# One decoder layer on eight cores: output and input in pieces, sample steps moved later, token segments joined, one normalisation paced

## The chip, the cores and the metric

The kernel runs on all 8 cores of one Trainium2 chip. Each core works on its own prompt of 2048 tokens and its own 16 sample sequences of one token each; there is no traffic between cores. The metric is the time on the device of the slowest core, in microseconds (us). Some executions fall in a slow state: the records of one die, or of both, show a lower granted TensorE clock (for example 0.923 to 0.926 on one die against 0.992 to 0.993 on the other). A median and the range in brackets are of all runs of a kernel, slow ones included; every ratio, and every profile read here, is of fast runs alone.

## The reference, cut to what matters

```python
# model width 1024, FFN width 2816, 4 GLA heads of 128 x 256
x = x + 0.5 * swiglu(rmsnorm(x, g_ffn1), w_ffn1_in, w_ffn1_out)      # "ffn1"
h = rmsnorm(x, g_mix)
u_a, v_a, q_b, k_b, v_b, g_b, lr_b, gate_a, gate_b = split(h @ w_in)
v_n = layernorm(gelu(v_a));  y_a = gelu(u_a) * (tril(W_s) @ v_n + b)  # "m1": spatial gating, chunks of 128
o, s_new = gla_recurrence(q, k, v, log_a, s0)                         # state (4, 128, 256) per sequence
y_b = rmsnorm_head(o) * silu(g_b)
mix = sigmoid(gate_a) * (y_a @ w_proj_a) + sigmoid(gate_b) * (y_b @ w_proj_b)
x = x + mix @ w_out
x = x + 0.5 * swiglu(rmsnorm(x, g_ffn2), w_ffn2_in, w_ffn2_out)      # "ffn2"
x = x + (p @ w_ple) * sigmoid(rmsnorm(x, g_ple) @ w_ple_gate)        # "ple"
y = rmsnorm(x, g_final)
```

For the 16 sample sequences of a core the recurrence is one step: a state of 512 KB is loaded, decayed, given `k^T v`, stored as an output, and multiplied by `q`. That makes 8 MB in and 8 MB out per core beside the weights.

## The kernel before

The prompt is cut into four subs of 512 tokens, worked in two pairs (A, B). In the first pair A carries the 16 sample tokens as well (528 columns, as segments of 256 and 272). For each pair the stages run in the order ffn1, m1 and the rest of the mixer, ffn2, ple; TensorE ("PE") takes its instructions in the order in which the host program emitted them (before, core 1, it stood 22.40 us until 906.02 in front of eight one-column matmuls that waited for a state copy, with matmuls of 512 columns behind them). The other engines are ACT (ScalarE: Square, Sigmoid, Ln, Exp and the like, with table loads in between: 78 of 1283 ns mean in the profile before), DVE (VectorE: element-wise work), POOL (GpSimd: some of the adds) and SP, which only issues transfers. Matmul results go to the banks of PSUM (`ps` in the profiles); the program lets ACT or DVE read a bank out (an "eviction") before PE writes it again. The "DMA share" is the mean busy share of the core's 16 DMA engines.

That order comes from a list scheduler. The main program emits the large matmuls ("foreground"). Everything else is a Python generator, spawned as a task, that yields the model time after which it wants to go on: norms, sample steps, the final norm with its stores. Before each foreground matmul group the tasks that are due are run:

```python
def pe(self, fn, reads, writes, dur):            # every group of matmuls goes through here
    if not self.in_bg:
        self.run_bg()                            # tasks due by now emit their instructions first
        ... # then: run further tasks for as long as the operands are not ready
    idx = p.add("pe", fn, reads, writes, dur=dur)
    ...
    return idx
```

The norm: ACT squares each chunk of x, DVE adds the squares, one matmul with ones sums over partitions, ACT makes Ln and Exp of it (1/rms), DVE multiplies eight chunks.

```python
def rinv_of(acc, segs, adds, dst=None):
    ...
    for (c0, n, _, _) in segs:                   # one round per token segment
        for t in adds[c0]:
            yield from after(t)
        ... # matmul with ones, ACT Ln, ACT Exp
    return r

def xn_of(S, gc, src, segs, r, pace=0.0):
    for (c0, n, _, _) in segs:
        yield K.until(r.k(0, c0, n), margin=-200.0)
        for kc in range(KC):                     # 8 multiplies on DVE
            K.stt(S.xn(kc, c0, n), src(kc, c0, n), col(gc + kc), r(0, c0, n), ALU.mult, ALU.mult, ...)
            if kc % 2:
                yield pace                       # 0: all eight in one burst
    ...
```

The sample steps share one state buffer for even and one for odd sequences. Their loads and stores, and the stores of y, go out on the queue of the SP engine, in order; here a transfer that waited held everything behind it (before, core 1: SP issued nothing from 851.76 to 876.32 us, 24.5 of it spent waiting for the y store to land).

```python
def samples():
    ...
    t0 = K.now                                   # spawned as pair 1 starts
    for n_ in range(NS):
        s0 = s0b[n_ % 2]
        yield max(K.until(s0.k(), ...), t0 + SPACE * (n_ + 1) - K.now)     # SPACE = 13500 ns
        ... # 4 matmuls k^T v, 4 DVE updates of s0
        K.dma("sp", ss_d[n_]..., s0.ap, ..., nbytes=524288)   # store the state
        K.act(snb.ap, s0.ap, AF.Copy, ...)                    # bf16 copy
        if n_ + 2 < NS:
            load_s0(n_ + 2)                                   # next load into the same buffer, at once
        ... # 8 one-column matmuls that read snb
```

The last task of a sub multiplies x and stores it; for the first pair in one piece, and reloads x for the next pair in one piece:

```python
def final_task(S, segs, chunked, nxt, adds, pace):
    ...
            for kc in range(KC):
                K.stt(S.x(kc, c0, n), ...)
                if chunked:
                    K.dma("sp", y_d[S.s][:, kc, ...], ...)
                yield pace
    ...
        if not chunked:
            K.dma("sp", y_d[S.s], S.x.ap[:, :, 0:PT], ..., nbytes=1 << 21)
        if nxt is not None:
            K.dma("sp", nxt.x.ap[:, :, 0:PT], x_d[nxt.s], ..., nbytes=1 << 21)
```

## Time and profile before

The median of five runs was 1669.62 us (1665.83 to 1878.98). The profiled execution was a fast one; its cores spanned 1658.0 to 1666.1 us at a mean granted clock of 0.979 to 0.984.

I split the span at the first matmul of each stage, recognised in the timeline by its operand tiles (for example, the first matmul that reads the low-rank weights begins m1). Medians over the eight cores:

| stage | length, us | of it PE idle, us |
|---|---|---|
| start, up to the first real matmul | 20.7 | 16.6 |
| pair 0: ffn1 | 239.9 | 0.0 |
| pair 0: m1 of A / of B | 21.7 / 18.2 | 2.8 / 0.0 |
| pair 0: rest of mixer and ffn2 | 477.0 | 9.6 |
| pair 0: ple | 37.4 | 3.5 |
| pair 1: ffn1 | 272.7 | 26.1 |
| pair 1: m1 of A / of B | 18.7 / 18.9 | 2.4 / 0.0 |
| pair 1: rest of mixer and ffn2 | 469.2 | 5.4 |
| pair 1: ple | 53.0 | 11.9 |
| after the last ple matmul | 13.2 | 12.6 |

Read it by comparing equal work: the two ffn1 stages differ by 33 us, though the first has 16 columns more to work on and the second only the sample steps beside it (16 times some 0.65 us of matmuls, about 10 us); the two ple stages differ by 16. This is the timeline of core 1 around the first m1, PE only (columns: start, duration, engine and line, operation, tiles, count, and in brackets the idle time before it with what ended it):

```profile
283.40 2.62 PE L45 MATMUL ps<-s_xn,s_wlr 128*16 128x512 bf16 x8 [2.67 <-DVE s_xn L472]
```

B's first m1 matmuls wait 2.67 us for B's normalised x.

### The profile page before, as it was taken

How to read it: one execution, taken by the hardware profiler on the slowest of the kernel's cores; microseconds unless marked ns; L12 is line 12 of the kernel's file. 1: busy time of each engine (PE TensorE's matmuls, PEld its weight loads, DVE VectorE, ACT ScalarE, POOL GpSimd, SP SyncE). 2: the span in 40 equal slices, each digit the busy share in tenths (PEclk: the TensorE clock that was granted, in tenths of full speed). 3: DMA queues.
4: the chain of work that ended last, by engine and by line, in shares of the span. 5: the costliest groups of instructions: out<-in, count | busy, mean ns of one | idle time of the engine just before them, and what ended most of it. 6: DMA issues, size and time to landing. Idle time of an engine off the chain costs nothing.

```text
span 1666.1 us, 23013 instructions; the slowest of 8 cores (1658.0 to 1666.1 us)
## 1 busy us (share of the span) xinstructions
PE 1572.5 (94%) x9323; PEld 878.3 (53%) x9323; DVE 676.8 (41%) x1311; ACT 557.2 (33%) x989; POOL 200.3 (12%) x279
## 2 busy tenths in 40 slices
PE   5999999999899999999984999999999999999985
PEld 4576764655664444444431444444454476667653
DVE  3322236545623521123941333465364263222256
ACT  3321123644722531113530222237355242111145
POOL 3000001101122000001500000010012210000023
PEclk9999999999999999999997999999999999999998
DMA  9753543440524872537497666525341291524403
GB/s 192 110 90 52 89 76 65 77 77 13 90 36 68 152 137 42 97 63 161 71 209 206 176 146 150 122 51 93 60 78 38 51 151 32 97 52 89 77 1 103
DMA packets 65501, 155.67 MB, mean 93 GB/s; under 512 B 6322, under 2 KB 28482, under 8 KB 57716
## 3 DMA queue, kind: packets, MB, share of 16 engines
q0 software_dynamic: 34304, 113.31, 40.2%
q1 hardware_dynamic: 30260, 39.76, 7.8%
q8 instruction: 73, 1.20, 0.3%
q10 hardware_dynamic: 832, 1.14, 0.2%
q14 instruction: 32, 0.26, 0.1%
HBM read 248.01 MB, written 17.40 MB: 159 GB/s over the span
## 4 chain that ended last, share of the span: by engine, by line
PE 83%; DMA 6%; DVE 5%; ACT 4%; issue 2%; ACTq 0%; SPq 0%; DVEq 0%
PE ps L393 48%; PE ps L45 35%; DMA y<-s_x 2%; DMA ss_out<-s_s 2%; DVE s_xn L472 2%; ACT L451 1%; ACT s_tmp L451 1%; DMA s_s<-st 1%; DMA s_x<-x 1%; DVE s_Sf L472 1%; DVE s_x L472 1%; DVE s_ar L472 0%; DVE s_acc L460 0%; ACT s_sq L451 0%; DVE s_tmp L460 0%
## 5 line engine op out<-in xcount | busy, mean ns | idle before, releaser
L393 PE MATMUL ps<-s_xn,s_ring 128*128 128x512 bf16 (+2 forms) x2896 | 613.5, 339 | 0.0
L45 PE MATMUL ps<-s_xn,s_ring 128*128 128x512 bf16 (+2 forms) x2448 | 523.7, 337 | 14.1 <-ACT s_tmp L451 6.5
L451 ACT ACTIVATE s_tmp<-ps 128x512 f32<-128x512 f32 (+2 forms) x448 | 224.9, 512 | 590.6 <-PE ps L393 558.6
L393 PEld LDWEIGHTS ps<-s_xn,s_ring 128*128 128x128 bf16 x2896 | 282.8, 99 | 216.5 <-issue 5.4
L393 PE MATMUL ps<-s_ar,s_ring 128*128 128x512 bf16 (+2 forms) x1957 | 378.3, 341 | 0.0
L45 PEld LDWEIGHTS ps<-s_xn,s_ring 128*128 128x128 bf16 x2448 | 238.9, 99 | 196.5 <-ACT s_tmp L451 8.5
L460 DVE TENSOR_TENSOR s_ar<-s_tmp,ps 128x512 bf16<-128x512 f32 (+1 forms) x220 | 127.7, 583 | 410.1 <-PE ps L393 376.4
L393 PEld LDWEIGHTS ps<-s_ar,s_ring 128*128 128x128 bf16 x1957 | 191.2, 98 | 153.7 <-issue 1.7
L451 ACT ACTIVATE s_sq<-s_x 128x512 bf16<-128x512 f32 (+3 forms) x159 | 83.3, 535 | 227.4 <-DVE s_x L472 207.7
L472 DVE SCALAR_TENSOR_TENSOR s_x<-ps,s_x 128x512 f32<-128x512 f32 (+1 forms) x120 | 70.1, 587 | 183.7 <-PE ps L393 183.7
L45 PE MATMUL ps<-s_ar,s_ring 128*128 128x512 bf16 (+2 forms) x603 | 128.7, 330 | 2.6 <-DVE s_ar L472 2.2
L451 ACT ACT_TABLE_LOAD x78 | 100.1, 1283 | 16.9 <-DMA s_x<-x 9.0
L480 POOL DMA_DIRECT2D s_ring<-w_ffn_in x60 | 41.4, 724 | 379.0 <-PE ps L393 372.3
L472 DVE SCALAR_TENSOR_TENSOR s_xn<-s_x,s_cols,s_rinv 128x512 bf16<-128x512 f32 (+2 forms) x144 | 82.0, 639 | 1.9 <-ACT s_rinv L451 1.9
L45 PEld LDWEIGHTS ps<-s_ar,s_ring 128*128 128x128 bf16 x603 | 58.3, 98 | 45.6 <-DVE s_ar L472 4.5
L460 DVE TENSOR_TENSOR s_acc<-s_acc,s_sq 128x512 bf16<-128x512 bf16 (+2 forms) x147 | 58.9, 402 | 37.0 <-ACT s_sq L451 36.7
L45 PE MATMUL ps<-s_ring,s_xn 128*128 128x512 bf16 (+1 forms) x280 | 64.1, 382 | 0.0
L463 POOL TENSOR_TENSOR s_x<-s_tmp,s_x 128x256 f32<-128x256 f32 (+2 forms) x48 | 47.8, 1012 | 86.5 <-DVE s_tmp L460 78.6
L472 DVE SCALAR_TENSOR_TENSOR s_tmp<-s_tmp,ps 128x512 f32<-128x512 f32 (+1 forms) x40 | 23.2, 581 | 79.8 <-PE ps L393 75.6
L451 ACT ACTIVATE s_ar<-ps 128x512 bf16<-128x512 f32 (+2 forms) x52 | 28.8, 563 | 72.8 <-PE ps L45 53.6
L480 POOL DMA_DIRECT2D s_ring<-w_ffn_out x24 | 12.8, 533 | 301.0 <-PE ps L393 301.0
L463 POOL TENSOR_TENSOR s_ar<-s_tmp,s_ar 128x512 bf16<-128x512 f32 (+1 forms) x40 | 38.3, 960 | 81.5 <-DVE s_tmp L472 81.5
(138 smaller groups left out, 841.2 us busy)
## 6 DMA issues: line engine op xcount, KB each, us to landing
s_ring<-w_ffn_in POOLq DMA_DIRECT2D x36, 1024.0 KB, 17.1
s_ring<-w_in POOLq DMA_DIRECT2D x24, 1024.0 KB, 10.8
s_ring<-w_ffn_out POOLq DMA_DIRECT2D x16, 1024.0 KB, 10.6
s_s<-st SPq DMA_DIRECT2D x16, 512.0 KB, 4.7
ss_out<-s_s SPq DMA_DIRECT2D x16, 512.0 KB, 8.6
s_ring<-w_ffn_out POOLq DMA_DIRECT2D x8, 768.0 KB, 10.3
s_ring<-w_ffn_in POOLq DMA_DIRECT2D x16, 256.0 KB, 15.4
s_ring<-w_ffn_in POOLq DMA_DIRECT2D x8, 512.0 KB, 6.6
```

The source lines that it names most:

```text
L45: ins = self._e.matmul(*a, **k)
L393: ins = e.matmul(o, l, r, start=s, stop=t)
L451: return self.p.add("act", lambda e: e.activation(out, in_, func, scale=scale, **kw), reads, writes, dur=dur)
L460: return self.dve(lambda e: e.tensor_tensor(out, a, b, op), reads, writes, self.size(out), rate)
L463: return self.p.add("pool", lambda e: e.tensor_tensor(out, a, b, op), reads, writes, dur=200.0 + 2.1 * self.size(out))
L472: return self.dve(lambda e: e.scalar_tensor_tensor(out, a, s, b, op0, op1), reads, writes, self.size(out))
L480: return self.p.add(eng, lambda e: e.dma_start(out=out, in_=in_, allow_slow_non_contiguous=slow), reads, writes, dma_sem=sem, extra=extra, ...
```

## The change

The intent was to smooth background work: no 2 MB bursts on the SP queue, the sample steps out of the way of that traffic, background tasks run more eagerly where the main program has short groups, fewer and wider small operations, no burst of eight normalisations in front of evictions, and an earlier start. The diff, cut to its core:

```diff
-SPACE = 13500.0
+SPACE = 12000.0
@@ pe(): eager rule
+        if not self.in_bg and p.stage.startswith(("ple", "m1")):
+            self.run_bg()
@@ norms: one wait and one operation for both token segments; pace for B ahead of ffn2 and ple
-            for (c0, n, _, _) in segs:
-                for t in adds[c0]:
-                    yield from after(t)
+            for t in adds:
+                yield from after(t)
+            for (c0, n, _, _) in segs:
 ...
-            for (c0, n, _, _) in segs:
-                yield K.until(r.k(0, c0, n), margin=-200.0)
+            c0, n = span(segs)
+            yield K.until(r.k(0, c0, n), margin=-200.0)
 ...
-                            sq_feed(adds[S.s, c0], acc_t[S.X], c, c0, n, S.x)
+                        sq_feed(adds[S], acc_t[S.X], c, *span(S.segs), S.x)
 ...
+                        norm_task(S, gnext, adds[S], 1200.0 if S.X == 1 and gnext == C_GPLE else 0.0)
 ...
+            norm_task(S, C_GFFN2, adds, 1200.0 if S.X == 1 else 0.0)
@@ m1: A's spatial step waits for B's norm
             def spat():
+                yield from after(other)
@@ samples(): later, and the next load after the copy's matmuls
-            t0 = K.now
+            t0 = K.now + 90000.0
 ...
-                if n_ + 2 < NS:
-                    load_s0(n_ + 2)
                 yield K.until(snb.k())
                 ... # the 8 one-column matmuls
+                if n_ + 2 < NS:
+                    yield 0.6 * SPACE
+                    load_s0(n_ + 2)
@@ final_task(): y and the reload of x in pieces of 256 KB; for the last B halves PE sums the squares
+                    K.dma("sp", y_d[S.s][:, kc, c0:c0 + np_], S.x(kc, c0, np_), ..., nbytes=512 * np_)
+                    if nxt is not None and kc > 0:
+                        reload(nxt, kc - 1)
                     yield pace
 ...
+                    pss = PS.alloc() if len(halves) > 1 else None
-                    final_task(S, sg, last, N, adds, 400.0 if last else 2500.0)
+                    final_task(S, sg, N, adds, 400.0 if last else 5000.0, pss)
@@ start: order of the first loads, samples last, weights behind the second piece of x
-        x0 = [load_x("sp", A, 0, 2, share=1.7)]
-        K.dma("act", tgs.ap, xs_d, "xis", writes=[tgs.k()])
-        x0 += [load_x("act" if k0 % 4 else "sp", A, k0, 2, share=1.7) for k0 in range(2, KC, 2)]
+        x0 = [load_x("act" if k0 % 4 else "sp", A, k0, 2, share=1.7) for k0 in range(0, KC, 2)]
+        K.dma("sp", tgs.ap..., xs_d..., "xis", writes=[tgs.k()])
 ... # norm_first(): prompt columns first, the sample columns' squares after them
```

## The prediction

> **What bounds the kernel now.** I read the page's head first, then the busy time in stretches of 20 us, then who TensorE (PE) waits for, the chain that ended last, and the timeline at the two worst places.
>
> ```profile
> span 1666.1 us, 23013 instructions; the slowest of 8 cores (1658.0 to 1666.1 us)
> PE 1572.5 (94%) x9323; PEld 878.3 (53%) x9323; DVE 676.8 (41%) x1311; ACT 557.2 (33%) x989; POOL 200.3 (12%) x279
> ```
>
> TensorE is the bound on average: in most stretches it is busy 20.00 of 20.00 us with 94 or so matmuls of 512 columns, one per 213 ns. The change removes no such matmul, so all it can win is the 1666.1 - 1572.5 = 93.6 us in which PE stands still, and the time in which PE runs at a lower clock. The stretches show where those are.
>
> ```profile
> core 1: us, PE busy (x) PEld busy (x) DVE busy (x) ACT busy (x) POOL busy (x), PEclk, DMA share, GB/s
> ...
> 280.00:300.00 20.00, 17.34 (x89) 7.86 (x87) 18.96 (x47) 4.61 (x9) 3.73 (x9) 0.91 0.13 34
> ...
> 880.00:900.00 20.00, 3.63 (x17) 1.47 (x15) 0.00 (x0) 0.00 (x0) 1.48 (x2) 0.71 1.03 235
> 900.00:920.00 20.00, 13.98 (x67) 6.15 (x68) 6.55 (x14) 4.70 (x7) 0.00 (x0) 0.77 0.73 243
> ...
> 1600.00:1620.00 20.00, 15.52 (x122) 12.36 (x121) 12.92 (x27) 11.13 (x26) 9.04 (x12) 0.89 0.00 1
> 1620.00:1640.00 20.00, 16.90 (x138) 13.59 (x136) 9.38 (x25) 15.78 (x36) 7.98 (x11) 0.94 0.03 9
> 1640.00:1660.00 20.00, 9.28 (x54) 6.09 (x54) 17.47 (x44) 7.86 (x20) 7.80 (x10) 0.74 0.43 139
> ```
>
> Around 880 every compute engine is nearly idle while the DMA share is 1.03: PE waits for a transfer. In the last 60 us DMA is empty and DVE, ACT and POOL are half busy: these are waits between engines. Who is waited for:
>
> ```profile
> PE ps L45 <- ACT s_snb L451: 27.6, 3, 22.4
> PE ps L45 <- ACT s_sq L451: 13.9, 3, 11.5
> PE ps L45 <- DVE s_xn L472: 11.2, 4, 4.2
> PE ps L45 <- DVE s_tmp L460: 10.1, 6, 4.0
> PE ps L45 <- ACT s_tmp L451: 7.7, 8, 2.2
> PE ps L45 <- DVE s_acc L460: 5.7, 2, 5.2
> ```
>
> The first row is the sample work: the bf16 copy of a sequence's state, made by ACT. The chain of waits says what that stood behind:
>
> ```profile
> 851.00 25.30 DMA y<-s_x
> 877.00 17.60 DMA ss_out<-s_s
> 894.67 8.46 DMA s_s<-st
> ```
>
> So the 2 MB store of y holds the SP queue until 876, the 2 MB reload of x goes out there, the state store behind it takes 17.6 us instead of its median 8.6, and only then may the next state load start. PE, which runs in program order, stands for 22.4 us in front of eight one-column matmuls. On the other cores the same row totals 19.8 to 28.4 us.
>
> The tail, from the timeline:
>
> ```profile
> 1610.23 6.01 DVE L472 SCALAR_TENSOR_TENSOR s_xn<-s_x,s_cols,s_rinv 128x512 bf16<-128x512 f32 x8
> 1616.65 0.41 PE L45 MATMUL ps<-s_ring 128*128 128x272 bf16 x1 [4.04 <-DVE s_tmp L460]
> 1617.08 1.06 PE L45 MATMUL ps<-s_xn,s_ring 128*128 128x256 bf16 x4
> 1617.93 1.06 PE L393 MATMUL ps<-s_xn,s_ring 128*128 128x256 bf16 x4
> 1658.40 0.39 PE L45 MATMUL ps<-s_acc,s_ones_b 128*128 128x256 bf16 x1 [5.19 <-DVE s_acc L460]
> ```
>
> Eight normalisations of the B half go through DVE in one burst, the evictions of A stand behind them, PE idles 4.04 us, and afterwards four 256-column matmuls start 0.85 us apart where they had 0.44: half clock.
>
> [...]the granted clock falls to 0.5 after the 4.04 us gap, for 6.8 us, and after the 22.4 us gap.[...] SP issues nothing between the y store at 851.00 and the reload at 876.32.[...] The trace has 78 loads of 1283 ns mean, seven of them in the last 65 us.
>
> **The change part by part** (core 1).
>
> *y stores and x reloads in pieces, sample steps later.* The first pair's y (2 x 2 MB) and the reloads (2 x 2 MB) become 32 pieces of 256 KB, one store and one reload per 5 us in place of two 2 MB bursts per half. The sample steps start 90 us later, at about 930 instead of 843, and come every 12 instead of 13.5 us; the next state load is issued 7.2 us after the step, when the 8.6 us store is nearly done, so SP no longer stands in front of it. Two halves overlapping ask for 2 x 105 = 210 GB/s for some 20 us; stretches at 235 to 243 GB/s exist, and the reload of x is not read before the output stage at about 1010. The stall of 27.6 us goes, and with it the slow clock: eight matmuls took 3.45 us after the first gap and about 3.1 after the second, against 1.73. That is 1.7 + 1.4 = 3.1. Sum -30.7.
>
> *Tail.* Idle there: 0.43 + 4.04 + 1.32 + 1.20 + 0.58 + 0.33 + 1.75 + 2.22 + 5.19 + 7.34 = 24.4 us, plus slow clock. (a) The B normalisation is paced 1.2 us per two tiles: the 4.04 goes down to about 1 and the 3 us of slow clock after it go: -6. (b) The two token segments of A share one wait, one square, one add and one final multiply (528 wide). The two pairs of Ln and Exp now follow each other, which saves two table switches of 1.28 us each; the gaps 1.32 and 1.20 hang on them: -2.5. (c) The squares of the last B halves are summed by TensorE in PSUM: 14 adds on DVE of 0.28 go, 16 matmuls of 256 columns come (16 x 0.107 = 1.7 us of PE). DVE is busy 17.47 of 20 us in that stretch and causes the gaps 0.58 + 0.33 + 1.75 + 2.22 = 4.9, with about 2.3 us of slow clock behind them: about -5 + 1.7. (d) The end chain, 5.19 + 7.34, keeps sigmoid, multiply, add, square, matmul, Ln, Exp, eight multiplies and a store; about -1, as a new table load may stand in it. Together -12.8; I take -12, because ACT (about 10 us of work per B half, against 8.5 on PE) then limits.
>
> *m1.* B's first matmul waits 2.67 us in pair one and 2.42 in pair two for B's normalised x. Background work now runs after each matmul group in this stage, ahead of the next Gelu, and A's spatial step waits for B's norm. I expect most of it back: -4.
>
> *First pair's ple stage.* Gaps 1.86 + 1.18 + 0.47 = 3.5; pacing takes the first: -2. The burst for the next pair's normalisation stays.
>
> *Start.* PE does real work from 22.18. The small sample input (64 B runs) moves from the front of ACT's queue to the end of SP's, and weights wait for the second x piece. The last x piece may land 1 to 1.5 us sooner; a sample square and eight small matmuls enter the chain, about +0.5: -0.7.
>
> *Given back.* The sample steps now run until about 1112, through m1 and into the gates of pair two, each with four DVE operations of 0.4 us, one ACT copy of 1.06 us and two PSUM banks beside the one they hold: +2.
>
> Sum: -30.7 - 12 - 4 - 2 - 0.7 + 2 = -47.4, so core 1 ends at 1618.7. Other cores lose less of the stall but start lower (core 0: 1658.0 - 19.8 - 3 - 16.7 = 1618.5), so the slowest is about 1619 to 1620. The reported time is some 1.7 us above the span (1667.81 against 1666.1) and the median another 1.8: about **1623 us**, 2.8% faster.
>
> **Rivals.** *The transfer wait comes back elsewhere:* the pieces, the ring weights (about 76 GB/s in this stage) and the first state loads collide at 820 to 860, or a state store is late under the 12 us spacing. For it: DMA shares above 1 at 780 and 840, and 113 us of SP waiting for state stores. Against it: the unchanged spacing of 13.5 us caused no wait on DMA after 940, at 0.40 to 0.84 DMA share. It would give back 10 to 20 us: 1635 to 1643. *DVE or ACT becomes the bound in m1 of pair two:* DVE is busy 15.97 of 20 us at 1100 to 1120 and one sample step adds about 2 us per 12. With fewer banks, 3 to 8 us: 1626 to 1631. *The tail is a latency chain that the change only reorders:* ACT's table loads remain and the extra square matmuls make PE wait in order for ACT's squares. Then the tail gives 3 and not 12: 1632. *The tail gets near TensorE's own need* (A 18 us, B 17 + 1.7): 6 us more than I count, 1617.
>
> **Range and chances.** The stall is the surest term, since its cause is gone and not only moved; the stall alone leaves about 1639. The tail adds 3 to 18 with good odds of over 6. So low 1609, high 1640. Two per cent is at about 1635 (0.98 x 1668): to miss it, a collision or a nearly empty tail is needed. Faster 0.85, same 0.14, slower 0.01.
>
> **What would show it.** PE waits on the bf16 state copy total under 2 us, no stretch between 840 and 940 has PE under 19 us, and the chain of waits has no y store in mid-kernel. Cores draw together (they spread 8 us now). PE idle after the last pair's output stage falls from 24.4 to about 14[...]. The waits for normalised x fall from 11.2 to about 5. PE busy stays near 1570. It is wrong if the state-copy wait reappears later, if waits on weights appear in the second pair, or if m1 of the second pair idles over 5 us.

## The result, and the profile after

The median went from 1668.12 us (16 runs, 1665.75 to 1930.09) to **1631.26 us** (9 runs, 1629.84 to 1844.05). The ratio is 0.9783, with a 95% interval of 0.9773 to 0.9793. Ratios here and below are the mean time of one kernel's fast runs over that of the other's of the same rounds, so not quite the ratio of the quoted medians.

The profiled run was fast: cores 1623.4 to 1629.4 us, clock 0.989 to 0.992. The head of its page:

```profile
span 1629.4 us, 22821 instructions; the slowest of 8 cores (1623.4 to 1629.4 us)
PE 1562.5 (96%) x9223; PEld 878.0 (54%) x9347; DVE 668.1 (41%) x1237; ACT 553.6 (34%) x958; POOL 204.0 (13%) x279
```

The span fell by 36.7 us while PE's busy time fell by only 10 (fewer slow matmuls, and this trace has recorded 100 matmuls fewer than the one before): what went is idle time. The slowest core is now core 0 instead of core 1. Who PE waits for there (columns: total us, times, longest):

```profile
PE ps L45 <- DVE s_sq L462: 9.6, 1, 9.6
PE ps L45 <- DVE s_tmp L462: 7.3, 6, 2.7
PE ps L45 <- ACT s_tmp L453: 6.7, 7, 2.2
PE ps L45 <- DVE s_ar L479: 5.9, 2, 3.4
PE ps L45 <- ACT s_sq L453: 5.4, 7, 1.3
PE ps L45 <- DVE s_xn L474: 4.0, 1, 4.0
...
PE ps L45 <- DMA s_ring<-w_ffn_in: 2.2, 2, 2.0
```

The former first row, the bf16 state copy with 27.6 us, is absent. The first row, 9.6 us, is the first square after the kernel's start. The two middle stretches that had PE at 3.63 and 13.98 of 20 us are full (columns: stretch, then busy us of PE, PEld, DVE, ACT, POOL, granted clock, DMA share, GB/s; core 0 after):

```profile
880.00:900.00 20.00, 19.89 (x92) 9.03 (x93) 4.12 (x6) 3.28 (x6) 1.40 (x2) 1.00 1.04 205
900.00:920.00 20.00, 19.89 (x92) 9.09 (x93) 3.95 (x6) 3.58 (x6) 0.00 (x0) 1.00 0.70 190
```

DMA is as full as it was (share 1.04 at 880). What changed is that PE has nothing to wait for from it.

But one place got worse. The waits for normalised x fell from 11.2 to 4.0 us, as I had wanted, while a row appeared that was not among the large ones before: 5.9 us on `s_ar` of line 479, the normalised v of m1. The timeline of core 0 there:

```profile
272.71 5.38 DVE L474 SCALAR_TENSOR_TENSOR s_xn<-s_x,s_cols,s_rinv 128x512 bf16<-128x512 f32 x8
...
279.63 0.77 DVE L479 TENSOR_SCALAR s_ar<-ps,s_mv,s_rstd 128x512 bf16<-128x512 f32 x1
280.45 1.09 PE L45 MATMUL ps<-s_xn,s_ring 128*128 128x272 bf16 x4 [3.45 <-DVE s_ar L479]
281.33 1.11 PE L393 MATMUL ps<-s_xn,s_ring 128*128 128x272 bf16 x4
```

(The second of the two waits in that row is 2.41 us, in the second pair.) B's eight normalisations now stand in front of the subtraction that frees a PSUM bank of A's v blocks. PE waits 3.45 us for the bank, and afterwards four matmuls of 272 columns start 0.88 us apart, half clock (the records grant 0.5 for 6.83 us). The old 2.67 us at B's first matmul is gone, but this is more than it was.

By stage (us, medians over eight cores; idle PE time in brackets where it matters):

| stage | before | after | difference |
|---|---|---|---|
| start | 20.7 (16.6) | 18.3 (14.1) | -2.4 |
| pair 0: ffn1 | 239.9 | 240.1 | +0.2 |
| pair 0: m1 of A | 21.7 (2.8) | 23.5 (3.5) | +1.8 |
| pair 0: m1 of B | 18.2 | 18.7 | +0.5 |
| pair 0: rest of mixer, ffn2 | 477.0 | 476.4 | -0.6 |
| pair 0: ple | 37.4 (3.5) | 37.3 (3.4) | -0.1 |
| pair 1: ffn1 | 272.7 (26.1) | 241.5 (1.9) | -31.2 |
| pair 1: m1 of A | 18.7 (2.4) | 20.1 (2.4) | +1.4 |
| pair 1: m1 of B | 18.9 | 20.6 | +1.7 |
| pair 1: rest of mixer, ffn2 | 469.2 (5.4) | 472.0 (5.1) | +2.8 |
| pair 1: ple | 53.0 (11.9) | 46.0 (8.0) | -7.0 |
| after the last ple matmul | 13.2 (12.6) | 12.7 (11.1) | -0.5 |
| sum | | | -33.4 |

The slowest core gained 36.7 because the cores also drew together a little (8.1 us apart before, 6.0 after). Some of the shifts are work moved, not time won: five of the sixteen sample steps now fall behind ffn1 of pair 1, each with about 0.65 us of matmuls, so some 3.3 us went from that stage to the two rows with +1.7 and +2.8.

### The profile page after: what moved, and what is told of

Its sections match the earlier page's. It is cut to its first block, busy times and chain, and to the rows that moved or that the text cites. A ratio compares the mean times of both kernels' runs of the same rounds, so it can differ in the third digit from the quotient of the medians.

```text
span 1629.4 us, 22821 instructions; the slowest of 8 cores (1623.4 to 1629.4 us)
## 1 busy us (share of the span) xinstructions
PE 1562.5 (96%) x9223; PEld 878.0 (54%) x9347; DVE 668.1 (41%) x1237; ACT 553.6 (34%) x958; POOL 204.0 (13%) x279
## 4 chain that ended last, share of the span: by engine, by line
PE 85%; DVE 6%; ACT 3%; DMA 3%; issue 2%; POOL 1%; DVEq 0%; ACTq 0%; POOLq 0%; SPq 0%
PE ps L393 48%; PE ps L45 36%; DVE s_xn L474 2%; ACT L453 2%; DMA s_s<-st 1%; ACT s_tmp L453 1%; DMA s_ring<-w_ffn_in 1%; DVE s_x L474 1%; DVE s_Sf L474 1%; DMA s_x<-x 1%; POOL s_x L465 1%; DVE s_tmp L462 0%; DVE s_ar L474 0%; DVE s_st L851 0%; DVE s_s L474 0%
## 5 line engine op out<-in xcount | busy, mean ns | idle before, releaser
L453 ACT ACTIVATE s_tmp<-ps 128x512 f32<-128x512 f32 (+3 forms) x448 | 225.1, 511 | 576.0 <-PE ps L393 553.2
L45 PEld LDWEIGHTS ps<-s_xn,s_ring 128*128 128x128 bf16 x2464 | 239.8, 98 | 206.8 <-ACT s_tmp L453 7.4
L453 ACT ACTIVATE s_sq<-s_x 128x512 bf16<-128x512 f32 (+2 forms) x133 | 79.5, 605 | 262.5 <-DVE s_x L474 232.4
L474 DVE SCALAR_TENSOR_TENSOR s_xn<-s_x,s_cols,s_rinv 128x512 bf16<-128x512 f32 (+3 forms) x120 | 82.9, 754 | 2.6 <-ACT s_rinv L453 2.6
L45 PEld LDWEIGHTS ps<-s_ar,s_ring 128*128 128x128 bf16 x607 | 58.9, 98 | 45.9 <-DVE s_ar L474 4.6
L45 PE MATMUL ps<-s_ring,s_xn 128*128 128x512 bf16 (+1 forms) x297 | 67.5, 379 | 0.5 <-issue 0.2
L462 DVE TENSOR_TENSOR s_acc<-s_acc,s_sq 128x512 bf16<-128x512 bf16 (+1 forms) x105 | 48.7, 464 | 32.7 <-ACT s_sq L453 32.4
## 6 DMA issues: line engine op xcount, KB each, us to landing
s_ring<-w_ffn_in POOLq DMA_DIRECT2D x36, 1024.0 KB, 17.7
```

The lines of the kernel that those rows point to most:

```text
L45: ins = self._e.matmul(*a, **k)
L453: return self.p.add("act", lambda e: e.activation(out, in_, func, scale=scale, **kw), reads, writes, dur=dur)
L462: return self.dve(lambda e: e.tensor_tensor(out, a, b, op), reads, writes, self.size(out), rate)
L474: return self.dve(lambda e: e.scalar_tensor_tensor(out, a, s, b, op0, op1), reads, writes, self.size(out))
```

## The experiments

What was disputed: whether the stall at 880 went because of the pieces or because of the delay; why m1 got worse; and which parts of the tail's change do anything. Twelve kernels ran. A difference of 0.1% between two of them is within their intervals, so for small effects I go by the stage table of the profiled fast run, whose unaffected stages repeat within about 1 us from kernel to kernel (ffn1 of the first pair: 239.9 to 240.8).

### 1. Before, with the sample steps 90 us later and nothing else

```diff
-            t0 = K.now
+            t0 = K.now + 90000.0
```

> The kernel before with one line changed: the sample steps start 90 us later (spacing stays 13.5 us, y and x stay 2 MB transfers). Theory (the steps stall only because they fall into the two 2 MB stores and two 2 MB reloads at 851 to 927): the wait of TensorE on the bf16 state copy falls from 20-28 us to under 3 us, time 1636 to 1642. Rival (the pieces are what cures it; whole transfers still collide with the first state loads and the weights): the wait stays above 10 us somewhere after 930, time 1650 or more.

Measured: median 1642.17 us (4 runs, 1638.94 to 1782.69), ratio 0.9835 (0.981 to 0.9861). Ffn1 of pair 1 took 236.7 us with 0.0 idle. Of the state-copy wait this is all that is left, on three of the eight cores (here core 5):

```profile
PE ps L45 <- ACT s_snb L451: 2.7, 1, 2.7
```

So one line gives some 27.5 of the 36 us (1668 x 0.0165 against 1668 x 0.0217). The mechanism that I had named is right (a state store and load behind a y store and a reload), but the 2 MB transfers may stay whole: it is enough that no sample step runs while they do.

### 2. Before, with the pieces and nothing else

```diff
-                        if chunked:
-                            K.dma("sp", y_d[S.s][:, kc, c0:c0 + np_], ...)
+                        K.dma("sp", y_d[S.s][:, kc, c0:c0 + np_], ..., nbytes=512 * np_)
+                        if nxt is not None and kc > 0:
+                            reload(nxt, kc - 1)
                         yield pace
... # the 2 MB store and the 2 MB reload are taken out; pace 5000 instead of 2500
```

> The kernel before with y stores and x reloads in 256 KB pieces, one of each per 5 us, and nothing else (steps still begin at about 843). Theory (time overlap of steps and bursts is the cause, so pieces alone only soften it): the wait on the bf16 state copy falls to 5 to 15 us, time 1645 to 1656. Rival (pieces alone are the cure): wait under 3 us, time 1636 to 1642. Second rival (pieces put SP in front of more waits, steps get later still): wait 20 us or more, time 1660 or more.

Measured: 1673.13 us (4 runs), ratio 1.0028 (1.001 to 1.0046): slightly slower than before. The wait was 29.5 to 34.8 us on all eight cores, against 19.8 to 28.4. Core 4's row, and from its timeline the steps' updates on DVE and the state's transfers on the SP queue:

```profile
PE ps L45 <- ACT s_snb L451: 34.8, 2, 18.2
```

```profile
831.65 1.65 DVE L472 SCALAR_TENSOR_TENSOR s_s<-s_s,s_aTs,ps 128x256 f32<-128x256 f32 x4
...
843.83 1.66 DVE L472 SCALAR_TENSOR_TENSOR s_s<-s_s,s_aTs,ps 128x256 f32<-128x256 f32 x4 [0.18 <-PE ps L45]
844.36 0.83 SPq L480 DMA_DIRECT2D ss_out<-s_s  x1
...
861.72 0.39 SPq L480 DMA_DIRECT2D s_s<-st  x1
...
880.72 0.51 SPq L480 DMA_DIRECT2D ss_out<-s_s  x1
```

The first state was ready to be stored at 833.3 us and its store went out at 844.36, 11.1 us later; the second was ready at 845.5 and its store went out 35.2 us later. Each piece of y waits for its multiply on DVE and each reload waits for its piece of y to have left, all in order on the one queue, with the state transfers between them. Taken over the first five stores of a core, they stood 93 to 102 us in the queue, against 68 to 82 before; in the kernel after it was 0. Between 840 and 922 us SP waited 43.9 us for y in six waits on this core, against 32.2 in two before. The 17.36 us from the first store to the load behind it are no such wait: the store took 17.30 us to land, and on every core each load went out within 0.1 us of the landing of its store. Why the store took that long, at a DMA share of 1.05 from 840 to 860, no run separates. The second rival of the expectation was right. The prediction had credited the pieces together with the delay; alone they do harm.

### 3. After, with 2 MB transfers again

```diff
-                    K.dma("sp", y_d[S.s][:, kc, c0:c0 + np_], ...); reload(nxt, kc - 1) per chunk, pace 5000
+                    first pair: one 2 MB store, then one 2 MB reload, pace 2500
```

> The changed kernel with the first pair's y stores and x reloads as whole 2 MB transfers again; the sample steps stay 90 us later. Theory after b_delay and b_chunk (the distance in time alone cures, pieces alone make it worse): 1629 to 1633, no wait on the state copy at the start of pair two. Rival (the pieces still spare the weights or the first steps something): 1635 or more, with new waits on ring weights between 820 and 930.

Measured: 1631.14 us (6 runs, 1629.83 to 1836.06), ratio 0.977 (0.9754 to 0.9785), ffn1 of pair 1 239.4 us with 1.8 idle, against 241.5 with 1.9. Once the steps start later, pieces or no pieces make no difference. With 1 and 2 this settles the largest term: the delay does it.

### 4. After, with the eager rule in ple only

```diff
-        if not self.in_bg and p.stage.startswith(("ple", "m1")):
+        if not self.in_bg and p.stage.startswith("ple"):
```

> The changed kernel with the eager background rule kept for the ple stage alone, not for m1. Theory (in m1 the rule puts B's burst of eight normalisations in front of A's four normalisations of v, which free the PSUM banks, so TensorE waits 3.45 and 2.41 us for banks instead of for B's norm): the gaps move back to B's first low-rank matmul (2.7 and 2.4 us), the first m1 A stage shrinks from 23.5 to about 22 us with no half clock after it, time 1628 to 1630. Rival (the gaps come from the later spatial step of A): nothing moves, 1631.

Measured: 1629.13 us (6 runs, 1627.95 to 1701.18), ratio 0.9767 (0.9746 to 0.9788). The gap went back to B's first m1 matmul (2.67 us in the first pair as expected, but only 1.12 instead of 2.4 in the second), and m1 of A took 21.7 and 18.2 us instead of 23.5 and 20.1. So the rule, in m1, does not take the wait away: it only runs B's norm earlier, in front of other DVE work that PE needs sooner.

### 5. After, with B's normalisation paced ahead of the mixer too

The change paces B's eight multiplies ahead of ffn2 and ple, but not ahead of m1.

```diff
-    norm_task(S, gnext, adds[S], 1200.0 if S.X == 1 and gnext == C_GPLE else 0.0)
+    norm_task(S, gnext, adds[S], 1200.0 if S.X == 1 else 0.0)
```

> The changed kernel with B's normalisation ahead of the mixer also paced, 1.2 us per two tiles, as it already is ahead of the other two stages. Theory (burst on DVE in front of the bank-freeing normalisations of v): both gaps of m1 A (3.45 and 2.41 us) fall under 1 us and the half clock goes, time 1623 to 1627. Rival (the Ln/Exp table switch between the Gelus, 2 x 1.28 us on ACT, delays the banks): the gaps stay above 2 us, time 1630 to 1632. Second rival (the paced norm comes too late): the gap reappears at B's first matmul.

Measured: 1626.47 us (4 runs, 1624.67 to 1628.42), ratio 0.9748 (0.9729 to 0.9766). M1 of A took 19.8 and 18.3 us, 3.7 and 1.8 less than after. PE on core 4:

```profile
275.97 0.64 PE L45 MATMUL ps<-s_xn,s_ring 128*128 128x272 bf16 x4 [0.79 <-DVE s_ar L479]
...
279.33 1.89 PE L45 MATMUL ps<-s_xn,s_wlr 128*16 128x512 bf16 x8
```

The bank is waited for 0.79 us instead of 3.45, four matmuls of 272 columns take 0.64 instead of 1.09, and B's first matmuls follow without a wait. With 4 this shows the cause: it was the burst, together with the rule that placed it early. The rule is worth having only with the pace.

### 6. After, without any pace

```diff
-    1200.0 if S.X == 1 and gnext == C_GPLE else 0.0     (ahead of ple)
+    0.0
-    norm_task(S, C_GFFN2, adds, 1200.0 if S.X == 1 else 0.0)
+    norm_task(S, C_GFFN2, adds)
```

> The changed kernel with both paced normalisations of B put back to bursts. The prediction's step (pacing takes the 4.04 us gap of the tail down to about 1 and the half clock behind it, and 2 us of the first ple stage): the last ple stage grows from 46 to about 51 us, the first from 37.3 to about 39, time 1636 to 1640. Rival (the merged squares and adds had already unloaded DVE, pacing only moves small gaps): both stages within 1 us, time 1630 to 1633.

Measured: 1634.24 us (5 runs, 1633.65 to 1900.99), ratio 0.9792 (0.9776 to 0.9807), unclear by the 2% line. The tail's gap is back, core 1:

```profile
1581.95 5.86 DVE L474 SCALAR_TENSOR_TENSOR s_xn<-s_x,s_cols,s_rinv 128x512 bf16<-128x512 f32 x8
...
1588.21 0.41 PE L45 MATMUL ps<-s_ring 128*128 128x272 bf16 x1 [4.10 <-DVE s_tmp L462]
```

The last ple took 49.8 instead of 46.0 us, the end 11.9 instead of 12.7: the pace is worth about 3 us in the tail, not the 6 I had put on it. Ple of the first pair stayed at 37.3, so the 2 us that I had put on the pace there do not exist.

### 7. After, squares of the last B halves summed by DVE again

```diff
-                    pss = PS.alloc() if len(halves) > 1 else None
+                    pss = None
```

> The changed kernel with the squares of the last two halves summed on DVE again instead of by TensorE in PSUM. The prediction's step (-5 from DVE, +1.7 of matmuls, a little in the end chain): last ple stage plus end grow by 3 to 5 us, time 1634 to 1637. Rival (ACT's table switches and evictions bound these halves, so DVE's adds were free): within 1 us, 1630 to 1632.

Measured: 1629.78 us (4 runs, 1628.88 to 1631.84), ratio 0.9766 (0.975 to 0.9783). The last ple took 44.2 instead of 46.0, the end 13.6 instead of 12.7: together 0.9 us less. Moving the adds to PE gained nothing. ACT's table loads show a cost that the prediction had not counted (core 2, whole kernel; 78 after):

```profile
L453 ACT ACT_TABLE_LOAD x76 | 97.5, 1283 | 10.4 <-DVE s_Sf L474 5.9 <-issue 2.5 <-DVE s_ar L462 0.5
```

From the first matmul of the last ple on there are five loads here, against seven after and seven before. A's two pairs of Ln and Exp stand between one pair of loads (1594.43 and 1597.63 us), where the kernel before had two pairs of loads. With the squares in PSUM, B's first half has its Ln and Exp early, between Sigmoids, for two loads more (after, core 0: 1607.62 and 1609.77).

### 8. After, with A's squares and final multiplies in ple per segment again

```diff
-                    sq_feed(adds, acc_t[S.X], c, *span(segs), S.x)
+                    for (c0, n, _, _) in segs:
+                        sq_feed(by[c0], acc_t[S.X], c, c0, n, S.x)
... # and the same for the final multiplies; the one joint wait ahead of them stays
```

> The changed kernel with A's squares and final multiplies of the ple stages split again into the 256 and 272 token segments; the two segments still share one wait before their Ln and Exp. Theory (the merged spans make the larger part of the tail's gain, since pacing alone gave 3 and the square matmuls nothing): the last ple stage plus end grow by 2 to 4 us, time 1633 to 1635. Rival (the common wait, which saves two table switches, is the gain and the width of the operations is nothing): within 1 us, 1630 to 1632.

Measured: 1634.66 us (7 runs, 1631.55 to 1851.37), ratio 0.9794 (0.9773 to 0.9815), unclear. The last ple took 49.5 (+3.5), the end 11.5 (-1.2): the joined operations are worth about 2.3 us. All fast runs lay between 1631.55 and 1634.66.

### 9. After, with the old start

The order of the first loads, the weights' gate and the first norm's order were put back; the rest stayed.

```diff
-        x0 = [load_x("act" if k0 % 4 else "sp", A, k0, 2, share=1.7) for k0 in range(0, KC, 2)]
-        K.dma("sp", tgs.ap..., xs_d..., "xis", writes=[tgs.k()])
+        x0 = [load_x("sp", A, 0, 2, share=1.7)]
+        K.dma("act", tgs.ap, xs_d, "xis", writes=[tgs.k()])
+        x0 += [load_x("act" if k0 % 4 else "sp", A, k0, 2, share=1.7) for k0 in range(2, KC, 2)]
... # extra=x0[0:1] for the first weights, and norm_first() as before
```

> The changed kernel with the start of the kernel before: sample input second on ACT's queue, sample columns inside the first squares, weights released by the first x piece. Theory (the start gives 2.4 us, three times the 0.7 predicted, since the x pieces land sooner and evenly): the start stage goes from 18.3 back to 20 to 21 us, time 1633 to 1634. Rival (the difference is noise of the first transfers from run to run): within 0.7 us.

Measured: 1632.8 us (5 runs, 1632.24 to 1861.14), ratio 0.9792 (0.9772 to 0.9812), unclear as a whole. The first real matmul came at 20.4 us as the median of the cores (19.3 to 23.7), against 18.3 (17.7 to 19.0) after and 20.7 before. So the new start gains about 2.1 us in that stage.

### 10. After, paced in three places: a version that turned out wrong

```diff
-    1200.0 if S.X == 1 and gnext == C_GPLE else 0.0
+    1200.0 if S.X == 1 else 0.0
-    final_task(S, sg, N, adds, 400.0 if last else 5000.0, pss)
+    final_task(S, sg, N, adds, (1200.0 if S is A else 400.0) if last else 5000.0, pss)
-    nxt.norm = K.spawn(xn_of(nxt, C_GFFN1, nxt.a["xp"], nxt.segs, nxt.rinv))
+    nxt.norm = K.spawn(xn_of(nxt, C_GFFN1, nxt.a["xp"], nxt.segs, nxt.rinv, 600.0))
```

The idea of the second edit came from the tail of experiment 5, where A's final multiplies make the same kind of burst (core 3):

```profile
1597.37 5.78 DVE L474 SCALAR_TENSOR_TENSOR s_x<-s_x,s_cols,s_rinv 128x528 f32<-128x528 f32 x7
```

> The changed kernel with three more bursts spread: B's norm ahead of the mixer paced 1.2 us (as in the run before), A's final multiplies in the last stage paced 1.2 instead of 0.4 us, the next pair's first normalisation paced 0.6 us. Theory (each gap left in the ple stages is an eviction standing behind a burst on DVE): the 2.69 us gap in the tail and the 1.43 us gap of the first ple stage fall under 1 us, time 1621 to 1625. Rival (ACT's table switches make those gaps, the bursts only follow them): as the run with the mixer pace alone, 1626 to 1627.

Measured: **the result is wrong** (relative error 0.385), and the time is 1641.22 us, ratio 0.9832. A miss in both respects. The 1/rms of the next pair (`s_s` below) lies in one of the sample steps' two state buffers, and the third edit lets the first state load overtake the multiplies that read it. The trace shows it on core 7: the first two state loads go out between 813.57 and 819.03 us; two of B's eight multiplies come before the second of them, and six after it had landed (timeline):

```profile
834.43 1.42 DVE L474 SCALAR_TENSOR_TENSOR s_xn<-s_ar,s_cols,s_s 128x512 bf16<-128x512 f32 x2 [15.22 <-DMA s_s<-st]
```

These six multiplied by a state instead of by 1/rms. So it is the program's order that is wrong. In ffn1 of pair 1 PE stood for 13.77 us (stage idle 14.0 us against 1.9) behind this same wait, so the run doesn't tell what the pace alone would be worth there.

### 11. The same without the wrong edit

Experiment 5, with the squares as in 7, and A's final multiplies paced at 800 instead of 400:

```diff
-    final_task(S, sg, N, adds, 400.0 if last else 5000.0, pss)
+    final_task(S, sg, N, adds, (800.0 if S is A else 400.0) if last else 5000.0, pss)
```

> The changed kernel with the pace ahead of the mixer (-5 us alone), DVE's adds in place of the square matmuls (-1 alone) and A's final multiplies in the last stage paced 0.8 instead of 0.4 us; without the pacing of the next pair's normalisation that made the earlier attempt wrong. Expected by sum: 1624 to 1626. If the final pace only pushes the end out, 1627 to 1628.

Measured: 1624.42 us (4 runs, 1624.01 to 1624.59), ratio 0.9741 (0.9722 to 0.9761), correct. But the tail did not profit: the last ple took 42.8 us and the end 16.4, together 59.2, against 58.7 in experiment 5 and 58.7 after. What leaves the ple stage comes back as a longer end chain. The gain over the changed kernel is that of the paced m1.

### 12. The same with the old spacing of the sample steps

What was left in ffn1 of pair 1 after the change was 1.9 us of idle PE, and it was a state load that came late. SP queue and timeline of core 7 after, around the place:

```profile
1012.04 0.37 SPq L482 DMA_DIRECT2D s_s<-st  x1
...
1035.56 1.66 DVE L474 SCALAR_TENSOR_TENSOR s_s<-s_s,s_aTs,ps 128x256 f32<-128x256 f32 x4 [3.98 <-DMA s_s<-st]
1037.40 0.41 DVE L462 TENSOR_TENSOR s_acc<-s_acc,s_sq 128x512 bf16<-128x512 bf16 x1
1037.86 0.39 PE L45 MATMUL ps<-s_acc,s_ones_b 128*128 128x512 bf16 x1 [2.27 <-DVE s_acc L462]
```

The step's update on DVE stands for the load, the sum of squares of A's norm stands behind it in DVE's order, and PE behind that. The DMA share is 1.00 in these microseconds (the FFN's output weights come in; same core):

```profile
1010.00:1020.00 10.00, 10.00 (x56) 4.61 (x55) 3.32 (x7) 1.26 (x2) 0.86 (x2) 1.00 1.00 158
```

The load is emitted 0.6 of the spacing after one step, for the step two spacings after that one; so the plan gives it 1.4 spacings, 16.8 us, while the one issued at 1012.04 was awaited until 1035.56. With 13.5 us between steps the plan gives 18.9, and asks for less bandwidth:

```diff
-SPACE = 12000.0
+SPACE = 13500.0
```

> The best version so far (a_best2) with the sample steps 13.5 us apart again, still 90 us later. Theory (at 12 us a state load meets the burst of output weights near 1020, DVE stands in front of it and TensorE waits up to 2.3 us for A's sum of squares): that wait goes, as in the run with the delay alone, first FFN of pair two 1.5 us shorter, time 1622 to 1624. Rival (the longer row of steps reaches further into the mixer, whose DVE is fuller): 1625 to 1627.

Measured: **1620.86 us** (5 runs, 1620.61 to 1622.41), ratio 0.9714 (0.97 to 0.9729), correct. Ffn1 of pair 1 went from 239.7 us with 1.7 idle to 236.7 with 0.0, and the cores lie within 1.2 us of each other (1618.1 to 1619.3). Of the 3.0 us in that stage some 0.65 are work moved, since one step more falls behind it (six instead of five). The run was on another chip than 11; the idle time of 0.0, and the ratio to the kernel before on the same chip, do not hang on that. This version beats both kernels; it keeps the delay, the eager rule, the joined segments and the new start, paces B's norm everywhere, and drops the square matmuls and the tighter spacing.

The stages of the runs that carry the argument, in us:

| | start | m1 of A, pair 0 | ple, pair 0 | ffn1, pair 1 | m1 of A, pair 1 | ple, pair 1 | end |
|---|---|---|---|---|---|---|---|
| before | 20.7 | 21.7 | 37.4 | 272.7 | 18.7 | 53.0 | 13.2 |
| after | 18.3 | 23.5 | 37.3 | 241.5 | 20.1 | 46.0 | 12.7 |
| 1: delay only | 21.0 | 21.7 | 37.4 | 236.7 | 19.2 | 53.5 | 13.2 |
| 2: pieces only | 21.1 | 21.7 | 37.4 | 276.9 | 18.7 | 52.6 | 13.4 |
| 3: no pieces | 18.0 | 23.4 | 37.4 | 239.4 | 19.4 | 47.1 | 13.1 |
| 4: eager in ple only | 18.1 | 21.7 | 37.4 | 239.8 | 18.2 | 45.9 | 12.7 |
| 5: paced m1 | 18.6 | 19.8 | 37.4 | 239.4 | 18.3 | 46.4 | 12.3 |
| 6: no pace | 18.3 | 23.5 | 37.3 | 240.9 | 19.4 | 49.8 | 11.9 |
| 7: no square matmuls | 18.2 | 23.5 | 37.4 | 241.3 | 19.4 | 44.2 | 13.6 |
| 8: split segments | 18.0 | 23.4 | 37.3 | 239.1 | 19.4 | 49.5 | 11.5 |
| 9: old start | 20.4 | 23.5 | 37.4 | 241.5 | 19.4 | 46.5 | 12.2 |
| 11: 5 and 7, A's final pace | 18.3 | 19.8 | 37.4 | 239.7 | 18.3 | 42.8 | 16.4 |
| 12: 11, spacing 13.5 | 18.8 | 19.8 | 37.4 | 236.7 | 18.3 | 42.7 | 16.6 |

## Why the prediction was right or wrong

The time lay in the predicted range and in the likeliest class, though 2.2% is close to the line of 2%; it was 8.3 us above the predicted 1623. One term carries the result: the stall makes 31.2 of the 33.4 us. Of the others m1 had the wrong sign, the first pair's ple gave nothing and the tail was over by 4.5 us. The sum behind it, -47.4 for core 1, was closer for that core (1666.1 to 1624.0, -42.1) than for the chip, because another core, with less of a stall to lose, became the slowest.

| term | predicted, us | measured, us (stages) |
|---|---|---|
| stall on the state copy, with its slow clock | -30.7 | -31.2, of it some 3.3 moved sample work |
| sample work given back | +2 | +4.5, of it the same 3.3 |
| m1 | -4 | +3.7 |
| first pair's ple | -2 | -0.1 |
| tail | -12 | -7.5 |
| start | -0.7 | -2.4 |

**The stall: right in size, and its mechanism right, but credited to two edits at once.** The step "become 32 pieces ... The sample steps start 90 us later" did not separate them. The delay alone brings ffn1 of pair 1 to 236.7 us (1); pieces alone raise the wait to 29.5 to 34.8 us (2); with the delay, taking the pieces out changes nothing (3). The predicted sign, no state-copy wait and no stretch between 840 and 940 with PE under 19 us, held on core 0. The first rival (the transfer wait comes back elsewhere) had a small truth: a state load late around 1035 under the 12 us spacing, 1.9 us instead of 10 to 20, and 12 shows that the spacing does it.

**M1: the step that failed.** I wrote that background work runs earlier and "I expect most of it back". It did run earlier, and the waits on normalised x fell to 4.0 us, even below the 5 that I gave as a sign. But that row is not the time. I had not asked what the earlier burst of eight multiplies, 5.38 us on DVE, would stand in front of: the subtraction that frees A's PSUM banks. The wait moved to another row (3.45 us, with 6.83 us of half clock). 4 shows that the eager rule moved it, 5 that the burst makes it. The same kind of burst is described in the prediction's tail, where it was the reason for the pace; in m1 I did not look whether the pace applied, and the diff excludes it there. The second rival had named DVE in m1 of pair 1 and a loss of 3 to 8 us. The loss was of that size, but in both pairs and from a burst, not from too much work: experiment 5 does the same DVE work without it.

**The tail: right in kind, too large in three of its parts.** (a) the pace: 6 predicted, about 3 measured (6). The stage gets the 4.10 us gap back, but the end chain is 0.8 us shorter then. (b) joined segments: 2.5 predicted, about 2.3 measured (8, which keeps the joint wait). The reason that I gave, two table loads of 1.28 us fewer for the joint wait, holds, though the total of 78 loads in both profiles hides it: 7 shows two loads fewer in the tail, and the squares in PSUM bring two back. (c) squares in PSUM: 3.3 net predicted; measured, taking them out gains 0.9 (7), which is within what these stages vary by, so: no gain. The prediction took DVE's load for the cause of the gaps and did not count ACT: two table loads more (2.6 us of ACT) come with this step, and PE then waits in its order for ACT's squares, 1.31 + 1.13 + 0.40 + 0.35 = 3.2 us after the last ple matmuls on core 0. So the third rival (the tail is a chain that is only reordered) was right on this part. The rest of the measured 7.5, about 3 us (7.5 - 3 - 2.3 + 0.9), is left for the joint wait, if parts that were taken away one at a time add up; no run takes the joint wait away. PE idle after the last output stage fell from 24.5 to about 19 us (8.0 + 11.1 in the stage table) and not to 14; on core 0 the longest gap before the very last matmuls was 2.69 us. 11 adds that ple and end must be read together: 3.2 us less in one was 3.7 more in the other. One slip of reading: the prediction calls DMA empty in the last 60 us, but its own last stretch has a share of 0.43; nothing rests on it.

**First pair's ple: the pace was put on a gap that the burst does not make.** Three gaps of 1.86, 1.18 and 0.47 us became 0.80, 1.43 and 1.21: reordered, same sum. 6 takes the pace away and the stage does not move.

**Start: underestimated.** 2.1 to 2.4 us came instead of 0.7. The spread over cores (18.8 to 22.2 us before, 17.7 to 19.0 after) shows that the order of the first loads mattered most on the worst cores, and I had reckoned with one core. One small cost beside it, on core 0 only: a wait of 1.97 us for the first weights at 22.6 us.

**Given back: right when the moved work is set off.** 4.5 - 3.3 leaves 1.2 us against 2.

## What to carry to other kernels

Before splitting a large transfer on an in-order queue, ask what its pieces wait for: here the pieces, which wait for computation, held the transfers between them longer than the whole transfer had (the first five state stores of a core 93 to 102 us in the queue, against 68 to 82), and moving the victim out of that time window did the whole job (ffn1 of pair 1 from 272.7 to 236.7 us by the delay alone). A buffer that is shared between a burst and a later load is safe only in the order that the burst happened to have: pace the burst, and check that order first. When a wait on one tile disappears from the table, look at the stage's length and not at that row, since an instruction that is run earlier stands in front of something (here 2.67 us of waiting for one tile became 3.45 us for another). Eager issue and pacing belong together: whoever emits a burst earlier must also thin it (the first m1 of A took 21.7 us before, 23.5 with the eager rule and no pace there, 19.8 with both).

## What the traces show of the clock, table loads, the SP queue and DVE's order

- Half clock: the records grant 0.5 for 3.41 us after gaps of 2.09 and 2.23 us (before, core 1, ended at 1333.42 and 434.49), and once with no gap over 1.05 us close before it (after, core 0, at 1224.65); around a gap of 2.69 us in the last ple they do so on core 1 of the kernel after and not on core 0. So in these traces the length of the gap alone does not decide. With all eight cores at work, a core's mean clock in the fast runs on record was 0.975 to 0.995; in slow-state runs it was, for example, 0.923 to 0.926 on one die in one of them, and 0.808 to 0.825 on all cores in the slowest (1954.4 us).
- Table loads: a load takes 1.28 us and the next operation begins 0.02 us after it, with the operation before it ending 0.01 us ahead (ACT of core 0 after):

```profile
1598.38 0.42 ACT L453 ACTIVATE s_sq<-s_x 128x256 bf16<-128x256 f32 x1
1598.81 1.28 ACT L453 ACT_TABLE_LOAD   x1
1600.11 0.38 ACT L453 ACTIVATE s_tmp<-ps 128x256 f32<-128x256 f32 x1
```

- Transfers that share the in-order SP queue with pieces that each wait for computation: SP waited 24.5 us ahead of the reload at 876.32 (before, core 1). With the pieces alone the first five state stores of a core stood 93 to 102 us in the queue, against 68 to 82 before, and PE's wait on the steps rose from 19.8 to 28.4 us up to 29.5 to 34.8.
- A transfer beside others: a store of 512 KB landed in 2.9 to 4.0 us as the first one of the kernel after, and in 16.3 to 19.1 us on all cores as the first one with the pieces alone, at a DMA share of 1.05 (core 4, 840 to 860).
- DVE's order and PSUM: B's eight multiplies, moved earlier there, delayed the evictions behind them, and 2.67 us of waiting for one tile became 3.45 us for another.
